# Three edits to the order in which results leave their PSUM banks in a two-layer encoder trunk

## The chip, the cores and the metric

The kernel runs on one core of one Trainium2 chip. The metric is the device time of one execution in microseconds (us); lower is better. The kernel before took 1122.87 us, the median of three runs (1122.69 to 1123.55).

## The reference

Two encoder layers work on x (512 tokens by 1024 features) in float32. Each layer normalises x by rows, projects it to queries, keys and values, lets every token attend to other tokens and to 256 memory rows, projects the heads back and adds the result to x; then comes a gated feed-forward block. The memory rows are normalised once, and each layer makes its own keys and values of them.

```python
mem_n = rms_norm(mem, mem_norm_g)
for i in range(DEPTH):                       # 2 layers
    h = rms_norm(x, g_mix_pre[i])
    proj = h @ w_in[i]                       # 12 query heads, 3 key and 3 value heads, 4 memory query heads
    tok = mixer_a(q, k, v, sink, ...) if i == 0 else mixer_b(q, k, v, qk_g, ...)
    mkv = mem_n @ w_mem_kv[i]                # 4 key heads and 4 value heads of 256 memory rows
    mo = memory_attention(qm, km, vm)
    o = jnp.concatenate([tok, mo], axis=-1) @ w_o[i]
    x = x + rms_norm(o, g_mix_post[i])
    h = rms_norm(x, g_ffn_pre[i])
    gu = h @ w_gate_up[i]
    f = (silu(gu[..., :D_FF]) * gu[..., D_FF:]) @ w_down[i]
    x = x + rms_norm(f, g_ffn_post[i])
```

Layer 0 (mixer A) turns a part of each key by position and limits attention to a band of tokens. Layer 1 (mixer B) normalises every query and key head by its own mean square, then turns it, and attends to all tokens.

## The kernel before, in words

**Numbers in two parts.** Every matmul operand is kept as two reduced float32 parts: a high part, made by a copy on ACT, and a low part, the difference of the source and the high part, made on DVE (`split`, lines 274 to 284; `split_scaled`, lines 286 to 293, also scales by a row factor r). A product is three matmuls: high by high, high by low, low by high (`mm3`, line 268).

**Who reads a bank.** Products and transposes end in PSUM banks. A bank is read by one engine at a time: where ACT and DVE both read it, the second waits for the first. A bank is free for TensorE (PE) again after the last reader.

**Order of the work.** PE issues in the order in which the program is traced. That order is a list written by hand, sorted by planned positions (`put` and `lay` in `mixer`, lines 659 to 740, with the constants `PACE`, line 37). The order on ACT, DVE, POOL and on SP, which issues all the loads, is chosen by the compiler: it plays the program through with modelled durations and, when an engine is free, takes the ready instruction that was traced first. Once chosen, each engine issues strictly in that order.

**The mixer's steps around the change.**

- `start` (line 1105) loads the inputs of layer 0 and sets up late steps: for x tiles 1 to 3 and for the two memory tiles (128 rows each), one call of `turned` and one of `factors`. `turned` (line 334) transposes one 128x1024 tile in two blocks of four 128x128 transposes; each block fills one of two banks with tag t (tile tp), and `split` then moves it into its high and low parts (mT for the memory). `factors` (line 324) squares the tile's two halves on ACT into a scratch tile (scr, tag tmp, two buffers) and makes the row factor.
- `kv_pieces` (line 452) makes keys and values of token tile t from one bank of 128x384. When the product is done it splits the values (vs, lines 471 and 286 to 293: a copy on ACT, the difference on DVE), then copies the keys on ACT (kx, line 473), turns them (`rope_a` or `rope_b`, on DVE, in layer 1 with a square on ACT and a factor on POOL), splits them (k, line 482) and copies the high part once more on POOL (line 402). `keys` (line 404) transposes them later.
- `q_pieces` (line 492) does the like for four query heads: copy qx on ACT (line 514 or 516), turn, split (q), transpose (line 534).
- `mem_pieces` (line 371) makes memory keys and values of tile m from a bank of 128x512: `split_scaled` for the keys (k), the POOL copy, `split_scaled` for the values (vm), so ACT, DVE, ACT, DVE read the bank in turn.

Layer 1 does not transpose the memory: layer 0 stores mT (line 688) and layer 1 loads it back (line 477, behind the kx copy on its queue).

Of the kernel before, what the change touches and what calls it, by code (L numbers as in the profile page):

```python
# [9 lines left out]
F32 = mybir.dt.float32  # L10
# [21 lines left out]
WPART = 2  # L32
BIG = 1e37
NFILL = 3
LOTS = ((0, 8), (8, 14), (14, 22))

PACE = [{'lag': 1.692, 'vlag': 0.479, 'jstep': 0.213, 'kstep': 0.375, 'klag': 0.742, 'qoff': [0.212, 0.126, 0.099], 'qlag': 1.02, 'late': 0.6, 'moff': -0.235, 'mdur': 0.562, 'mlag': 0.697, 'kw': [0, 0, 2, 0], 'mw': [2, 1, 1, 0], 'qw': [1, 0, 0, 1, 3, 3, 3, 3], 'hoff': 0, 'ow': [10.3, 10.8, 12.2, 13.2], 'ox': 11.4, 'od': 0.3, 'hstep': 0.872, 'hlag': 1.742, 'hjstep': 0.135, 'hvlag': 0.751, 'owm': [0, 0, 0, 0, 0, 0, 0, 0], 'q0step': 0.27, 'q0off': -0.032, 'q0lag': 0.919, 'm0off': -0.078, 'm0dur': 0.002, 'm0lead': 1.887, 'mlead': 1.201, 'qlead': 0.921, 'q0lead': 1.555, 'qstep': 1.002, 'tw': [0, 0, 0, 0, 0, 0, 0, 0], 'h2off': 0}, {'lag': 1.824, 'vlag': 0.535, 'jstep': 0.218, 'kstep': 0.777, 'klag': 1.715, 'qoff': [-0.027, -0.162, -0.027], 'qlag': 1.189, 'late': 2.15, 'moff': -0.088, 'mdur': 0.384, 'mlag': 1.205, 'kw': [0, 0, 0, 0], 'mw': [0, 0, 0, 0], 'qw': [0, 0, 0, 0, 0, 3, 1, 1], 'hoff': 0, 'ow': [10.2, 10.7, 12.2, 13.2], 'ox': 11.3, 'od': 0.3, 'hstep': 0.946, 'hlag': 1.847, 'hjstep': 0.295, 'hvlag': 0.568, 'owm': [0, 0, 0, 0, 0, 0, 0, 0], 'q0step': 0.718, 'q0off': -0.018, 'q0lag': 1.136, 'm0off': -1.059, 'm0dur': 0.171, 'm0lead': 2.465, 'mlead': 3.162, 'qlead': 1.895, 'q0lead': 1.42, 'qstep': 0.998, 'tw': [0, 0, 0, 0, 0, 0, 0, 0], 'h2off': 0.016}]
# [142 lines left out]
class Trunk:  # L180
# [93 lines left out]
    def split(self, hi, lo, src, pool=0):  # L274
# [8 lines left out]
        else:  # L283
            nc.vector.tensor_sub(lo, src, hi.bitcast(F32))  # L284

    def split_scaled(self, hi, lo, src, r, pool=0):

        nc = self.nc
        if pool & 2:
            nc.gpsimd.tensor_scalar(hi, src, r, 1.0, op0=OP.mult, op1=OP.mult)  # L290
        else:
            nc.scalar.activation(hi, src, AF.Copy, scale=r)
        nc.vector.scalar_tensor_tensor(lo, src, r, hi.bitcast(F32), op0=OP.mult, op1=OP.subtract)
# [35 lines left out]
        self.mean_square(xt[:, 512:], ss[:, 1:2], scratch())  # L329
        self.rstd2(r, e, ss[:, 1:2])  # L330

    def turned(self, h, his, los, t, nq=4):

        for b in range(2):
            tp = self.ps.tile([P, 4, P], F32, tag="t", name="tp", bufs=2)
            for k in range(4):
                self.nc.tensor.transpose(tp[:, k], h[:, (4 * b + k) * P:(4 * b + k + 1) * P], self.ident)
            k0 = 4 * b
            sl = (slice(None), slice(k0 % nq, k0 % nq + 4), slice(t * P, (t + 1) * P))
            self.split(his[k0 // nq][sl], los[k0 // nq][sl], tp)  # L340

    def scale_rows(self, rs, by_row=False):
# [27 lines left out]

    def mem_pieces(self, l, mk, put, x0, dx, lag, xw):

        w, ps = {}, []
        for u in range(4):
            self.unit(self.a["wm"][l, u], self.side(l, "mw", u), put=put, x=xw[u], dst=w, key=u,
                      g=self.gcol[:, 1, 2 * u:2 * u + 2])

        def prod(u, m):
            if u == 0:
                ps.append(self.tagged("s"))  # L380
            for k in (2 * u, 2 * u + 1):
                ms = (slice(None), k, slice(m * P, (m + 1) * P))
                c = slice((k % 2) * 512, (k % 2) * 512 + 512)
                self.mm3(ps[m], self.mT[:, 0][ms], self.mT[:, 1][ms], w[u][0][:, c], w[u][1][:, c],
                         k == 0, k == KD - 1)
            if u < 3:
                return
            kv = ps[m].rearrange("p (z h d) -> p z h d", z=2, d=HD)
            k2 = self.core.tile([P, 4, 3 * HD], F32R, tag="q2", name="k2", bufs=3)
            r = self.rm[:, m:m + 1]  # L390
            self.split_scaled(k2[:, :, :HD], k2[:, :, HD:P], kv[:, 0], r)
            self.again(k2)
            self.split_scaled(mk["v"][:, m, :, :HD], mk["v"][:, m, :, HD:], kv[:, 1], r)
            put(x0[3] + dx[3] + m * dx[3] / 2 + lag, lambda: self.keys(k2, mk["a"], mk["b"], m, 4))

        for u in range(4):
            for m in range(2):
                put(x0[u] + m * dx[u] / 2, lambda u=u, m=m: prod(u, m))
# [53 lines left out]
    def kv_pieces(self, l):  # L452
# [6 lines left out]
        def prod(t, st, u):  # L459
            self.ready(t)  # L460
            if u == 0:
                st["ps"] = self.tagged("acc" if t < 2 else "s")
            ps = st["ps"]
            for k in (2 * u, 2 * u + 1):
                c = slice((k % 2) * 384, (k % 2) * 384 + 384)
                self.mm3(ps[:, :384], self.hslice(0, k, t * P, t * P + P), self.hslice(1, k, t * P, t * P + P),
                         w[u][0][:, c], w[u][1][:, c], k == 0, k == KD - 1)
            if u == 3:
                kv = ps[:, :384].rearrange("p (z h d) -> p z h d", z=2, d=HD)
                r = self.rs[:, t:t + 1]  # L470
                self.split_scaled(self.vs[:, t, :, :HD], self.vs[:, t, :, HD:], kv[:, 1], r)
                kx = self.core.tile([P, 4, HD], F32, tag="qx", name="kx", bufs=3)
                ins = nc.scalar.activation(kx[:, :NG], kv[:, 0], AF.Copy, scale=r).ins
                if l:
                    with self.tc.issue_after(ins):
                        z, ks = t // 2, slice(t % 2 * 4, t % 2 * 4 + 4)
                        nc.sync.dma_start(self.mT[:, z, ks].bitcast(F32), self.spill[:, z, ks])
                r = self.rope(l, kx, t, NG, 1)
                if l:
                    nc.vector.tensor_mul(kx[:, :NG], kx[:, :NG], r[:, :NG, None].to_broadcast([P, NG, HD]))  # L480
                st["k2"] = self.core.tile([P, 4, 3 * HD], F32R, tag="q2", name="k2", bufs=3)
                self.split(st["k2"][:, :NG, :HD], st["k2"][:, :NG, HD:P], kx[:, :NG])
                self.again(st["k2"][:, :NG])
# [621 lines left out]
    def start(self, mkp):  # L1105
# [3 lines left out]
        with ExitStack() as st:  # L1109
# [41 lines left out]
            for t in range(1, NT):  # L1151
                late[t] = lambda t=t: (self.turned(x[t], *self.hT, t), factors(t, scr))
            for m in range(2):
                late["m", m] = lambda m=m: (self.turned(mh[m], [self.mT[:, 0]], [self.mT[:, 1]], m, KD),
                                            self.factors(mh[m], self.rm[:, m:m + 1], scr))
        return late

# [100 lines left out]
```

## Time and profile before

| what | value |
|---|---|
| median of three runs | 1122.87 us |
| the profiled execution, device time | 1122.94 us |
| its span, first to last instruction | 1121.1 us |
| PE busy | 1096.3 us, 98% of the span |
| DVE, ACT, POOL busy | 838.8, 660.6, 203.6 us |
| mixer of layer 0, with its start | about 0 to 170 us |
| mixer of layer 1 | about 545 to 757 us |
| granted TensorE clock | full in every slice |

The rest of the span is the two feed-forward blocks. Times below are microseconds from the start of the span. In a timeline, a row gives start, length, engine, source line, operation, tiles written and read, shape and count; a bracket at its end says how long the engine sat idle before it and what ended that.

### The profile page before, as it was taken

The numbers are of one execution on the slowest core, as the hardware profiler recorded it, in microseconds if no ns is written. First come the engines' busy times: TensorE is split into PE (matmuls) and PEld (weight loads), VectorE is DVE, ScalarE is ACT, GpSimd is POOL, SyncE is SP. The second block draws the span as 40 slices with busy tenths as digits, with TensorE's granted clock in tenths as the row PEclk, the third lists the DMA queues.
The fourth block names the chain that finished last, engine by engine and source line by source line (L and its number), as shares of the span: only waits on it lengthen the run. The fifth ranks groups of instructions, "written<-read, shape, count | busy, mean of one in ns | idle before, by whom it ended". The sixth has DMA issues, their size and how long they took to land.

```text
span 1121.1 us, 19499 instructions
## 1 busy us (share of the span) xinstructions
PE 1096.3 (98%) x7463; PEld 1005.2 (90%) x7463; DVE 838.8 (75%) x1399; ACT 660.6 (59%) x1343; POOL 203.6 (18%) x348
## 2 busy tenths in 40 slices
PE   9999999999999999999999999999999999999997
PEld 7899988899889989998898888878999899899985
DVE  5688885999547777885788988758995478669854
ACT  6678984666445634663467888756664355346631
POOL 5693331202000000000343552212000000000001
PEclk9999999999999999999999999999999999999999
DMA  6521015433753372325543221145136223422243
GB/s 237 198 84 40 20 57 215 161 132 118 242 178 113 118 278 76 113 78 196 179 151 113 76 76 39 38 164 175 46 107 210 73 79 113 147 66 101 84 165 113
DMA packets 38685, 139.29 MB, mean 124 GB/s; under 512 B 4416, under 2 KB 4800, under 8 KB 38464
## 3 DMA queue, kind: packets, MB, share of 16 engines
q1 hardware_dynamic: 38448, 137.91, 36.6%
q8 instruction: 58, 0.95, 0.3%
q14 instruction: 35, 0.29, 0.1%
q10 hardware_dynamic: 144, 0.14, 0.0%
HBM read 119.16 MB, written 18.87 MB: 123 GB/s over the span
## 4 chain that ended last, share of the span: by engine, by line
PE 70%; DVE 5%; ACT 3%; POOL 2%; issue 1%; DVEq 0%; POOLq 0%; ACTq 0%
PE ps L990 12%; PE ps L991 12%; PE ps L992 12%; PE ps L271 10%; PE ps L270 10%; PE ps L272 9%; PE tp L619 2%; PE o L634 1%; PE o L633 1%; PE s L558 1%; PE s L559 1%; POOL r L299 1%; DVE wlo L284 1%; ACT whi L280 1%; ACT junk L303 0%
## 5 line engine op out<-in xcount | busy, mean ns | idle before, releaser
L280 ACT ACTIVATE whi<-raw 128x1024 fp32r<-128x1024 f32 (+2 forms) x186 | 157.9, 863 | 183.2 <-PE ps L992 82.0
L284 DVE TENSOR_TENSOR wlo<-raw,whi 128x1024 fp32r<-128x1024 f32 (+2 forms) x178 | 175.4, 996 | 76.4 <-ACT whi L280 73.0
L990 PE MATMUL ps<-sf,whi 128*128 128x256 f32 x640 | 179.8, 281 | 0.2
L991 PE MATMUL ps<-sf,wlo 128*128 128x256 f32 x640 | 179.9, 281 | 0.0
L992 PE MATMUL ps<-sf,whi 128*128 128x256 f32 x640 | 179.8, 281 | 0.0
L270 PE MATMUL ps<-whi,f 128*128 128x512 f32 x352 | 137.2, 390 | 0.0
L271 PE MATMUL ps<-wlo,f 128*128 128x512 f32 x352 | 137.1, 390 | 0.0
L272 PE MATMUL ps<-whi,f 128*128 128x512 f32 x352 | 137.0, 389 | 0.0
L992 PE MATMUL ps<-a,whi 128*128 128x256 f32 x480 | 134.4, 280 | 0.0
L990 PE MATMUL ps<-a,whi 128*128 128x256 f32 x480 | 134.3, 280 | 0.0
L991 PE MATMUL ps<-a,wlo 128*128 128x256 f32 x480 | 133.9, 279 | 0.0
L990 PEld LDWEIGHTS ps<-sf,whi 128*128 128x128 f32 x640 | 121.1, 189 | 1.1 <-ACT p L996 0.6
L991 PEld LDWEIGHTS ps<-sf,wlo 128*128 128x128 f32 x640 | 121.3, 190 | 0.5
L992 PEld LDWEIGHTS ps<-sf,whi 128*128 128x128 f32 x640 | 121.4, 190 | 0.0
L308 POOL TENSOR_SCALAR e<-sso 128x1 f32<-128x1 f32 x8 | 3.4, 422 | 566.6 <-ACT junk L303 566.4
L270 PE MATMUL ps<-whi,hT 128*128 128x256 f32 (+1 forms) x320 | 98.8, 309 | 0.0
L271 PE MATMUL ps<-wlo,hT 128*128 128x256 f32 (+1 forms) x320 | 93.8, 293 | 2.4 <-DVE wlo L284 1.9
L609 POOL TENSOR_SCALAR p<-p,rd 128x256 f32<-128x256 f32 (+2 forms) x128 | 76.5, 619 | 99.6 <-DVE rd L606 41.9
L272 PE MATMUL ps<-whi,hT 128*128 128x256 f32 (+1 forms) x320 | 93.7, 293 | 0.0
L990 PEld LDWEIGHTS ps<-a,whi 128*128 128x128 f32 x480 | 90.4, 188 | 0.2
L991 PEld LDWEIGHTS ps<-a,wlo 128*128 128x128 f32 x480 | 90.4, 188 | 0.2
L992 PEld LDWEIGHTS ps<-a,whi 128*128 128x128 f32 x480 | 90.1, 188 | 0.0
(199 smaller groups left out, 2732.3 us busy)
## 6 DMA issues: line engine op xcount, KB each, us to landing
raw<-in_wgu_dram SPq DMA_DIRECT2D x48, 512.0 KB, 4.3
raw<-in_wd_dram SPq DMA_DIRECT2D x44, 512.0 KB, 4.5
rb<-in_wgu_dram SPq DMA_DIRECT2D x40, 512.0 KB, 3.6
raw<-in_wo_dram SPq DMA_DIRECT2D x17, 512.0 KB, 3.6
raw<-in_wq_dram SPq DMA_DIRECT2D x16, 512.0 KB, 4.8
xt<-x SPq DMA_DIRECT2D x12, 512.0 KB, 4.4
raw<-in_wm_dram SPq DMA_DIRECT2D x8, 512.0 KB, 3.8
x<-y SPq DMA_DIRECT2D x8, 512.0 KB, 3.0
```

The lines of the kernel that those rows point to most:

```text
L270: mm(out, lh, rh, start=first, stop=False)
L271: mm(out, lh, rl, start=False, stop=False)
L272: mm(out, ll, rh, start=False, stop=last)
L280: nc.scalar.activation(hi, src, AF.Copy)
L284: nc.vector.tensor_sub(lo, src, hi.bitcast(F32))
L299: g.tensor_tensor(r, r, self.mhalf[:, :r.shape[1]], op=OP.pow)
L558: nc.tensor.matmul(s[:, :n], qi, hd["ka"]()[:, k0 * P:k1 * P], start=True, stop=False)
L609: self.pooled = nc.gpsimd.tensor_scalar(hd["p"][z][:, :n], hd["p"][z][:, :n], rd[:, z:z + 1], 1.0, op0=OP.mult, op1=OP.mult)
L619: nc.tensor.transpose(tp[:, z], hd["p"][i][:, jj * P:(jj + 1) * P], self.ident)
L990: mm(out, wh[:, s], rh, start=start and k == 0, stop=False, skip_group_check=True)
L991: mm(out, wl[:, s], rh, start=False, stop=False, skip_group_check=True)
L992: mm(out, wh[:, s], rl, start=False, stop=k == 3, skip_group_check=True)
```

## The change

1. In `kv_pieces` the copy kx of the keys is traced ahead of the split of the values, in both layers, for all four token tiles.
2. In `mem_pieces` the two high parts (keys, values) are made first, both on ACT, and then the two low parts, both on DVE; the POOL copy is traced after all four. Both layers, two tiles each.
3. `turned` takes an argument `by`. For the two memory tiles it is the scratch allocator of `factors`: a copy on ACT, traced 150 places earlier in priority, moves the bank into a float32 scratch tile in SBUF, and both parts are then split from that tile. This adds four copies of 128x512 on ACT, in layer 0 only. No DMA is added or removed.

```diff
+URGENT = 150
+    def urgent(self):
+        return self.tc.high_priority(URGENT)

-    def turned(self, h, his, los, t, nq=4):
+    def turned(self, h, his, los, t, nq=4, by=None):
             sl = (slice(None), slice(k0 % nq, k0 % nq + 4), slice(t * P, (t + 1) * P))
+            if by is not None:
+                x = by().rearrange("p (k n) -> p k n", n=P)
+                with self.urgent():
+                    self.nc.scalar.activation(x, tp, AF.Copy)
+                tp = x
             self.split(his[k0 // nq][sl], los[k0 // nq][sl], tp)

     def mem_pieces(self, l, mk, put, x0, dx, lag, xw):
-            self.split_scaled(k2[:, :, :HD], k2[:, :, HD:P], kv[:, 0], r)
+            his, los = [k2[:, :, :HD], mk["v"][:, m, :, :HD]], [k2[:, :, HD:P], mk["v"][:, m, :, HD:]]
+            for z in range(2):
+                nc.scalar.activation(his[z], kv[:, z], AF.Copy, scale=r)
+            for z in range(2):
+                nc.vector.scalar_tensor_tensor(los[z], kv[:, z], r, his[z].bitcast(F32), op0=OP.mult, op1=OP.subtract)
             self.again(k2)
-            self.split_scaled(mk["v"][:, m, :, :HD], mk["v"][:, m, :, HD:], kv[:, 1], r)

     def kv_pieces(self, l):
-                self.split_scaled(self.vs[:, t, :, :HD], self.vs[:, t, :, HD:], kv[:, 1], r)
                 kx = self.core.tile([P, 4, HD], F32, tag="qx", name="kx", bufs=3)
                 ins = nc.scalar.activation(kx[:, :NG], kv[:, 0], AF.Copy, scale=r).ins
+                self.split_scaled(self.vs[:, t, :, :HD], self.vs[:, t, :, HD:], kv[:, 1], r)

     def start(self, mkp):
-                late["m", m] = lambda m=m: (self.turned(mh[m], [self.mT[:, 0]], [self.mT[:, 1]], m, KD),
+                late["m", m] = lambda m=m: (self.turned(mh[m], [self.mT[:, 0]], [self.mT[:, 1]], m, KD, scr),
                                             self.factors(mh[m], self.rm[:, m:m + 1], scr))
```

## Rows read from the trace of the kernel before

**Rows 1.** The profile's page, busy time by engine: PE.
```profile
PE 1096.3 (98%) x7463; PEld 1005.2 (90%) x7463; DVE 838.8 (75%) x1399; ACT 660.6 (59%) x1343; POOL 203.6 (18%) x348
```
**Rows 2.** Who PE waited for, whole span: us in total, times, longest us.
```profile
PE ps L271 <- DVE wlo L284: 1.9, 2, 1.1
...
PE tp L337 <- DVE mT L284: 1.4, 1, 1.4
...
PE tp L534 <- DVE q L284: 0.5, 1, 0.5
```
**Rows 3.** Timeline, layer 0, all engines: the memory's transposes and what surrounds them.
```profile
28.17 2.18 ACT L280 ACTIVATE whi<-raw 128x512 fp32r<-128x512 f32 x4
...
28.87 5.51 POOL L282 TENSOR_TENSOR wlo<-raw,whi 128x512 fp32r<-128x512 f32 x4
...
29.31 1.44 DVE L284 TENSOR_TENSOR k<-kx,k 128x192 fp32r<-128x192 f32 x1
...
30.25 1.06 ACT L280 ACTIVATE mT<-tp 128x512 fp32r<-128x512 f32 x2
30.86 1.29 DVE L284 TENSOR_TENSOR mT<-tp,mT 128x512 fp32r<-128x512 f32 x2
...
31.61 1.25 PE L337 MATMUL tp<-cst,mh 128*128 128x128 f32 x8 [1.40 <-DVE mT L284]
...
32.62 0.47 PE L270 MATMUL ps<-whi,mT 128*128 128x512 f32 x1
...
33.16 0.40 PE L272 MATMUL ps<-whi,mT 128*128 128x512 f32 x1
```
**Rows 4.** Timeline, layer 0: bank of token tile 2's keys and values.
```profile
24.55 0.42 ACT L292 ACTIVATE vs<-ps,rs 128x192 fp32r<-128x192 f32 x1 [0.48 <-PE ps L272]
...
25.45 0.42 ACT L473 ACTIVATE kx<-ps,rs 128x192 f32<-128x192 f32 x1
...
27.90 0.36 ACT L280 ACTIVATE k<-kx 128x192 fp32r<-128x192 f32 x1 [2.03 <-DVE kx L428]
```
**Rows 5.** Low parts (line 284) and float32 copies (line 153): ns min/median/max, first and last start us.
```profile
L284 DVE TENSOR_TENSOR k<-kx,k x8: 348/359/1437, 17.6 to 583.4; 128x192 fp32r<-128x192 f32 x8
L284 DVE TENSOR_TENSOR mT<-tp,mT x4: 676/686/693, 30.9 to 35.9; 128x512 fp32r<-128x512 f32 x4
...
L153 ACT ACTIVATE as<-tp x8: 586/598/616, 199.4 to 771.8; 128x512 f32<-128x512 f32 x8
```
**Rows 6.** Chain of waits, layer 1, 548 to 615 us: start us, us, what.
```profile
563.53 0.42 ACT vs L292
563.95 0.32 ACT kx L473
...
579.27 0.33 DVE vs L293
...
595.33 0.69 DVE wlo L284
```
**Rows 7.** Timeline, layer 1, ACT.
```profile
561.75 0.43 ACT L292 ACTIVATE vs<-ps,rs 128x192 fp32r<-128x192 f32 x1
...
575.55 0.41 ACT L292 ACTIVATE vs<-ps,rs 128x192 fp32r<-128x192 f32 x1
...
579.64 0.42 ACT L473 ACTIVATE kx<-ps,rs 128x192 f32<-128x192 f32 x1
...
583.23 0.46 ACT L514 ACTIVATE qx<-ps,rs 128x256 f32<-128x256 f32 x1
```
**Rows 8.** Timeline, layer 1: DVE's low parts of weights, PE's products.
```profile
571.13 2.90 DVE L293 SCALAR_TENSOR_TENSOR wlo<-raw,cst,whi 128x512 fp32r<-128x512 f32 x4 [0.17 <-ACT whi L292]
...
573.28 0.39 PE L271 MATMUL ps<-wlo,mT 128*128 128x512 f32 x1
...
581.80 0.28 PE L272 MATMUL ps<-whi,hT 128*128 128x256 f32 x1
```
**Rows 9.** Timeline, layer 0, ACT: the last square of a memory half.
```profile
21.48 0.64 ACT L303 ACTIVATE scr<-mh 128x512 f32<-128x512 f32 x1
```

More of the change, by code (lines that the diff above doesn't have):

```diff
@@ L371, in mem_pieces @@
     def mem_pieces(self, l, mk, put, x0, dx, lag, xw):
+        nc = self.nc
         w, ps = {}, []
```

## The prediction

> **What bounds the kernel now.** I read the page first: PE is busy 1096.3 of 1121.1 us [rows 1], so all that a change of order can win is PE's idle time, some 25 us over the whole span, and only the part of it that hangs on the moved instructions. So the second view is the list of who PE waited for. Three of its entries touch the moved work [rows 2]: 1.4 us, once, in which a transpose waits for a low part of mT; 1.9 us, two waits for low parts of weights, the longer one 1.1 us; and 0.5 us in which a transpose waits for a query's low part. The third view is the timeline around each, to see who was late, and the fourth the chain of waits in layer 1.
>
> The first wait stands in layer 0. PE has filled both banks with the first memory tile's transposes and cannot start the second tile's until DVE has read the first bank (the 1.40 us) [rows 3]. The bank was full long before. Its ACT copy stood behind four weight copies, which run from 28.17 to 30.35, and only then follow mT's high parts at 30.25 and its low parts at 30.86. Those weight copies are themselves late: ACT sat idle for 2.03 us before the key copy that stands ahead of them [rows 4], because the keys were turned late.
>
> In layer 1 the chain that ends in the wait for a weight's low part at 595.33 comes out of the keys: it passes a copy of values on ACT (0.42 us), the copy of keys behind it, and a low part of values on DVE (0.33 us) [rows 6].
>
> **Edit 1, keys first.** No instruction is added. In layer 0 the key copy of tile 2 starts at 25.45, 0.90 us after the bank could first be read at 24.55: it stands behind the values' copy and, as the bank has one reader at a time, behind their low part on DVE [rows 4]. Keys first, it can start 0.90 us earlier, and so can the turn, the key's high part and the weight copies behind it. No wait of PE ends at these keys; the 0.90 us counts only in edit 3. The values' own parts come 0.42 us later; what hides it is the query products, which all stand ahead of the first head that reads values.
>
> In layer 1 the same order costs more: tile 0's values leave at 561.75, but its keys only at 563.95, since ACT had been given the next tile's values in between [rows 6, 7]; tile 3's values leave at 575.55 and its keys at 579.64, 4.1 us later [rows 7]. DVE is nearly full there, so not all of that comes back. What certainly leaves the chain are the two steps on values, 0.42 + 0.33 = 0.75 us [rows 6]. What can come back at most before the next thing is late: the first query copy starts at 583.23, and its product ends about 581.80 + 0.28 = 582.08 [rows 7, 8]; so 1.15 us. I take the middle, 0.9 us off PE's waits. Bounds: 0, if POOL's factor or DVE's order sets the chain anyway, and 1.6 us, the 1.1 us and the 0.5 us waits whole [rows 2]. Next late thing: the query chains, one after the other on ACT.
>
> **Edit 2, the memory's high parts first.** Four banks, the same four instructions each. ACT no longer waits for DVE between its two copies, and the keys' low part comes one copy later: 0.46 us, by the query copy of the same 128x256 (the last row) [rows 7]. PE transposes these keys only after further query products, which are the cover; without it 0.46 us per tile would show. PE's list of waits has none for these parts. I count 0, and 0.5 us either way for the range.
>
> **Edit 3, the memory's rows leave by a copy.** Four copies of 128x512 into float32 are added on ACT, 0.598 us each by the nearest row [rows 5], 2.4 us together. With them a bank is free after one ACT instruction instead of an ACT and a DVE instruction. If ACT reaches it only at 30.25 as now, the bank is free at 30.85 instead of 31.55 (30.86 + 0.69): 0.7 of the 1.40 us go. With the 0.90 us of edit 1, or with the copies' priority ahead of one or two of the four weight copies, all 1.40 us go.
>
> But the wait has a successor: PE's first product with mT starts at 32.62, its third matmul, at 33.16, 0.54 us later, reads the low part [rows 3]. The path to it is now copy, copy, high part, low part: 3 x 0.60 + 0.69 = 2.5 us from when ACT turns to it. From 29.35 (30.25 less 0.90) the low part ends at 31.84, so the product may start at 31.3, a gain of 1.3 us. From 30.25 it ends at 32.74, and the gain is 0.4 us.
>
> The low part is also made from another place. Now one of its two operands is in PSUM, and all four took 0.68 to 0.69 us although POOL was busy beside them [rows 3, 5]. The low part of the keys, whose two operands are both in SBUF, took 0.36 us as a rule, and 1.44 us at 29.31, under the same POOL pieces [rows 3, 5]. The Trainium skill (SBUF — State Buffer, section Who interferes with whom) says that a DVE instruction with two SBUF inputs contends with a GpSimd instruction that reads SBUF, that whoever starts first holds the shared port for its whole instruction, and that with at most one SBUF input there is no contention; by that rule all four new low parts are exposed, which speaks against this edit, and the trace agrees as far as the 1.44 us goes. POOL's four pieces here are 5.51 / 4 = 1.38 us each [rows 3]. One low part behind a whole piece ends 1.38 us later: from 29.35 at 33.2, and the product starts at 32.7, a loss of 0.1 us; from 30.25, a loss of 1.0 us. With undisturbed low parts the whole sum (with layer 1's 0.9 us) would be 1120.7 us; with one POOL piece ahead of each, 1122.1 us.
>
> So the edit is worth between -1.4 and +1.0 us; I take -0.6, halfway between the 1.3 us gain and the 0.1 us loss from 29.35, since edit 1 makes that start the likely one. The moved squares of the memory rows (below) I count at 0. A gain at 32 us reaches the end because PE is the bound nearly everywhere behind it.
>
> **The sum**: -0.6 - 0.9 + 0 = -1.5 us against the profiled execution's 1122.94 us (its span of 1121.1 and 1.8 us around it), so 1121.4 us. That execution stands 0.07 us above the median of the runs. About 0.2% of the time, 2.25 us, is what a measurement of this kernel can tell from no change; so 1120.6 to 1125.1 counts as the same.
>
> **Rivals.**
>
> *Both waits go whole* (chance 0.31). The copies overtake the weight copies, low parts meet no POOL piece, and keys come early enough to clear the query transposes too: -1.4 - 1.6 - 0.5 = -3.5 us, 1119.4 us. For it: the keys of tile 3 have 4.1 us to win [rows 7]. Against: the longer mT path, and DVE, which has little room around 575 us.
>
> *Each wait gets a successor* (0.21). The product waits for mT as long as the transposes waited for the bank, and in layer 1 POOL's factors and DVE's order set the chain's end: 0, so 1122.9 us. This is also how it looks if the scheduler, which plays the program with modelled durations, puts the instructions back where they were, so that the change does not do what it says.
>
> *Slower: the low parts meet POOL* (0.12). Place: layer 0, 30 to 38 us. In the worst order three low parts in a row (both blocks of the first memory tile, the first of the second) each wait for one of the four POOL pieces: high part done at 30.25 + 1.8 = 32.05, then 3 x (1.38 + 0.69) = 6.2 us, so 38.3. The second tile's product, six matmuls of 0.27 us behind the first [rows 3], needs it at 32.62 + 1.6 + 0.54 = 34.8. PE stands still for 3.5 us; with layer 1's -0.9 that is +2.6, 1125.5 us. It decides from when the second tile's first low part ends after 34.8. For it: the 1.44 us row. Against: the keys' median stayed at 0.36 us [rows 5], and POOL, once delayed, is out of the way sooner than in this worst order. It is what the rule of the Trainium skill named above would give if it held three times in a row.
>
> Two smaller ones I fold into these. The squares of the memory rows end at 22.1 now [rows 9], and they share their two buffers with the new copies; handed out in traced order, they would wait for the low parts and put four squares of 0.64 us, 2.6 us of ACT work, into 31 to 38 us. And in layer 1 the four low parts of memory weights run from 571.13 to 574.03, the first needed by 573.28 [rows 8]: at 0.73 us each, the first is done at 571.86, so 1.4 us of key work can go ahead of them free, and more shows in PE one to one.
>
> **How the numbers follow.** My forecast has 0.36. With the successor rival's 0.21 the time is the same with 0.57; faster by over 0.2% 0.31; slower 0.12. The likeliest case's own range, from its bounds, is 1120.6 to 1122.9. For 8 in 10 the range goes down to 1118.9, half a microsecond under the whole gain, as orders elsewhere shift too, and up to 1124.2, the worst of edit 3's ordinary bounds (+1.0) with edit 2's 0.5 against and nothing won in layer 1, less 0.2 us, as the three seldom meet.
>
> **What would show it.** Right: the transposes at about 30 us start without the 1.40 us wait; each bank of the memory is read by ACT alone; the first product with mT starts 0.3 to 1.3 us earlier; kx starts as the product ends in all eight banks; the wait at 595 us is shorter. Step by step wrong: a wait of the mT product for low parts as long as the old one (edit 3), low parts of mT above 0.69 us (the port), the wait at 595 us unchanged although the keys are early (edit 1), a new wait near 573 us, squares of the memory rows after 30 us. The forecast as a whole is wrong if PE's idle time changes in the heads or the feed-forward blocks, where nothing is edited, by more than it does here.

## The result, and the profile after

The kernel after takes 1127.97 us (median of six runs), the kernel before, run beside it, 1122.91 us: a ratio of 1.0047, 95% interval 1.0037 to 1.0056, so 5.1 us slower. The prediction said 1121.4 us, range 1118.9 to 1124.2. It is wrong in sign, and the result lies outside its range. The profiled execution took 1127.67 us, with a span of 1125.7 us against 1121.1.

The page's row of busy times by engine, to be set beside [rows 1]:

```profile
PE 1097.7 (98%) x7463; PEld 1005.7 (89%) x7463; DVE 839.7 (75%) x1399; ACT 662.4 (59%) x1347; POOL 202.3 (18%) x348
```

ACT has its four instructions more (1347 instead of 1343). PE is busy 1.4 us longer with the same 7463 instructions: some of them were slower. The list of who PE waited for, whole span (us in total, times, longest us), against [rows 2]:

```profile
PE ps L271 <- ACT mT L281: 5.4, 1, 5.4
...
PE ps L272 <- DVE wlo L285: 1.3, 2, 0.8
...
PE ps L273 <- DVE mT L285: 0.2, 1, 0.2
```

The 1.4 us wait of the transposes is gone and so is the 0.5 us wait of the query's transposes. The weights' low parts cost 1.3 instead of 1.9 us. But there is a wait that was nowhere before: 5.4 us, once, in which a product waits for a *high* part of mT, made by ACT. The timeline of layer 0, all engines, shows where it comes from; its first rows answer to [rows 3].

```profile
27.06 2.20 ACT L281 ACTIVATE whi<-raw 128x512 fp32r<-128x512 f32 x4 [0.40 <-PE ps L273]
...
28.16 6.44 POOL L283 TENSOR_TENSOR wlo<-raw,whi 128x512 fp32r<-128x512 f32 x4
...
29.16 1.06 ACT L348 ACTIVATE scr<-tp 128x512 f32<-128x512 f32 x2
...
29.80 1.13 PE L342 MATMUL tp<-cst,mh 128*128 128x128 f32 x8
30.12 1.15 ACT L281 ACTIVATE mT<-scr 128x512 fp32r<-128x512 f32 x2
30.78 2.69 DVE L285 TENSOR_TENSOR mT<-scr,mT 128x512 fp32r<-128x512 f32 x2 [0.69 <-ACT mT L281]
...
30.89 0.47 PE L271 MATMUL ps<-whi,mT 128*128 128x512 f32 x1
...
31.83 0.50 PE L273 MATMUL ps<-whi,mT 128*128 128x512 f32 x1 [0.23 <-DVE mT L285]
...
32.63 0.40 PE L273 MATMUL ps<-whi,mT 128*128 128x512 f32 x1
33.39 1.27 DVE L439 TENSOR_TENSOR rt<-kx,cst 128x48 f32<-128x48 f32 x1
33.86 0.61 ACT L308 ACTIVATE scr<-mh 128x512 f32<-128x512 f32 x1
...
34.47 0.61 ACT L308 ACTIVATE scr<-mh 128x512 f32<-128x512 f32 x1
...
35.08 1.05 ACT L348 ACTIVATE scr<-tp 128x512 f32<-128x512 f32 x2
...
37.52 0.36 ACT L281 ACTIVATE k<-kx 128x192 fp32r<-128x192 f32 x1 [1.07 <-DVE kx L442]
37.79 1.13 ACT L281 ACTIVATE mT<-scr 128x512 fp32r<-128x512 f32 x2
...
38.43 1.29 DVE L285 TENSOR_TENSOR mT<-scr,mT 128x512 fp32r<-128x512 f32 x2 [0.16 <-ACT mT L281]
...
38.45 0.80 PE L271 MATMUL ps<-whi,mT 128*128 128x512 f32 x1 [5.43 <-ACT mT L281]
...
39.05 0.63 PE L272 MATMUL ps<-wlo,mT 128*128 128x512 f32 x1
```

The first memory tile goes as the prediction had it: the copies come off at 29.16, the second tile's transposes start at 29.80 without a wait (31.61 before), and the first product starts at 30.89 instead of 32.62. Then the *second* tile, whose transposes are done by 30.93, stands still. Its copies run only at 35.08, behind four weight copies (32.24 to 33.95) and two squares (scr<-mh) that lay before 22.1 us in the kernel before [rows 9]. Its high parts run only at 37.79, behind the keys' high part (37.52), which waited for DVE to turn the keys. PE starts the second tile's product at 38.45.

The products behind the wait are slow: 0.63 us each instead of 0.40. The same kernel's busy time by stretch (stretch in us, its length, busy time and count of PE, PEld, DVE, ACT, POOL, granted TensorE clock, DMA share, GB/s) says why:

```profile
34.00:38.00 4.00, 0.00 (x0) 0.00 (x0) 3.87 (x9) 2.93 (x9) 3.28 (x7) 0.76 0.40 140
...
38.00:42.00 4.00, 3.55 (x8) 2.78 (x9) 1.57 (x3) 2.79 (x7) 1.41 (x4) 0.50 0.90 328
42.00:43.00 1.00, 1.00 (x4) 0.77 (x3) 0.00 (x0) 0.62 (x2) 0.83 (x1) 0.55 0.62 262
43.00:45.00 2.00, 2.00 (x12) 1.66 (x11) 0.00 (x0) 0.06 (x1) 1.71 (x2) 1.00 1.17 492
```

While PE had nothing to do, its granted clock fell to 0.50, the 1.2 GHz level, and it stayed there through 38 to 42 us of products; from 43 us it is 2.4 GHz again.

In layer 1 the change did what it should. The timeline there, ACT and PE, against [rows 7, 8]:

```profile
581.02 0.41 ACT L486 ACTIVATE kx<-ps,rs 128x192 f32<-128x192 f32 x1
...
588.64 0.47 ACT L528 ACTIVATE qx<-ps,rs 128x256 f32<-128x256 f32 x1 [0.69 <-PE ps L273]
...
600.95 0.39 PE L272 MATMUL ps<-wlo,hT 128*128 128x256 f32 x1 [0.53 <-DVE wlo L285]
```

The whole program is some 6.3 us late at that point. So the keys of tile 3, at 581.02, come 4.9 us earlier than before (579.64 + 6.3 - 581.02), and the first query copy 0.9 us earlier (583.23 + 6.3 - 588.64).

PE's 7463 instructions come in the same order in both kernels, so each can be set beside itself. The difference in start time grows and shrinks as follows: -0.43 us before the memory's transposes (the start of the program, no work of the change), -1.38 where their wait is gone, +0.48 at the first product's low part, +5.70 at the second tile's high part, +1.95 during the slow products, -1.43 in layer 1 (nearly all of it at two places, near 592 and 596 us of the kernel before), -0.30 in many small steps behind. The sum is +4.59 us, the 4.6 us of the spans. Such differences compare one execution of each kernel.

### The profile page after: what moved, and what is told of

It is laid out like the page before. It is cut to its first block, busy times and chain, and to the rows that moved or that the text cites. A ratio compares the mean times of both kernels' runs of the same rounds, so it can differ in the third digit from the quotient of the medians.

```text
span 1125.7 us, 19514 instructions
## 1 busy us (share of the span) xinstructions
PE 1097.7 (98%) x7463; PEld 1005.7 (89%) x7463; DVE 839.7 (75%) x1399; ACT 662.4 (59%) x1347; POOL 202.3 (18%) x348
## 4 chain that ended last, share of the span: by engine, by line
PE 69%; DVE 5%; ACT 2%; POOL 2%; issue 2%; DMA 1%; POOLq 0%; DVEq 0%; SPq 0%; ACTq 0%
PE ps L1004 12%; PE ps L1006 12%; PE ps L1005 12%; PE ps L272 10%; PE ps L271 10%; PE ps L273 10%; PE tp L633 2%; PE o L648 1%; PE o L647 1%; PE s L572 1%; PE s L573 1%; POOL r L304 1%; DVE wlo L285 1%; POOL p L623 0%; ACT whi L281 0%
```

## The experiments

The first two take the change apart.

**Edits 1 and 2 without edit 3.** The memory's rows are split from their banks again:

```diff
-late["m", m] = lambda m=m: (self.turned(mh[m], [self.mT[:, 0]], [self.mT[:, 1]], m, KD, scr),
+late["m", m] = lambda m=m: (self.turned(mh[m], [self.mT[:, 0]], [self.mT[:, 1]], m, KD),
```

> Edits 1 and 2 alone, the memory tiles split from their banks as before. All theories: the 5.4 us wait for mT goes, since nothing stands between the bank and the parts. The bank wait of 1.4 us comes back, but shorter, about 0.7 us, because the weight copies already ran 1.1 us earlier (27.06 against 28.17). If the 1.4 us won in layer 1 belong to the key order, they stay: 1122.9 - 0.7 - 1.4 = 1120.8 us. If they came only from layer 0 being late, the time is 1122.2 us or more.

Measured: 1121.55 us, ratio 0.9991 [0.9981, 1.0000]. Who PE waited for between 27 and 44 us:

```profile
PE tp L342 <- DVE mT L285: 1.1, 1, 1.1
PE ps L273 <- DVE mT L285: 0.6, 1, 0.6
```

The time lies between the two forecasts. The old bank wait is back, 0.3 us shorter, with a 0.6 us successor; by PE's start times layer 0 is some 0.5 us worse than before, and layer 1 gains its 1.5 us without the copies.

**Edit 3 alone.** The kernel before, with the copies and the argument `by` of the change and nothing else of it:

```diff
-late["m", m] = lambda m=m: (self.turned(mh[m], [self.mT[:, 0]], [self.mT[:, 1]], m, KD),
+late["m", m] = lambda m=m: (self.turned(mh[m], [self.mT[:, 0]], [self.mT[:, 1]], m, KD, scr),
```

> Edit 3 alone, keys and memory rows as before. Theory buffers (the second memory tile's copies wait for scratch buffers that the squares of the first tile hold, and those wait for the first tile's low parts): the wait of PE is there without edits 1 and 2, 5.4 us or up to 0.9 us more since the keys come later, and layer 1 wins nothing: 1129 to 1130.5 us. If the wait needs the new key order (ACT standing behind a key part), it is under 3 us and the time under 1126.

Measured: 1128.56 us, ratio 1.0057 [1.0043, 1.0071]. Who PE waited for between 27 and 44 us:

```profile
PE ps L271 <- ACT mT L281: 3.9, 1, 3.9
```

The loss comes with edit 3 alone, and layer 1 gains nothing. The wait lies between the two forecasts. The keys' high part is not ahead of the second tile's here (it is behind it, at 38.08), and 3.9 us of wait remain; the squares are at 34.16 and 34.77 and the copies at 35.38, as in the change.

**Edit 2 alone.** The kernel before, with the order of `mem_pieces` of the change and nothing else of it:

```diff
-self.split_scaled(k2[:, :, :HD], k2[:, :, HD:P], kv[:, 0], r)
+his, los = [k2[:, :, :HD], mk["v"][:, m, :, :HD]], [k2[:, :, HD:P], mk["v"][:, m, :, HD:]]
+for z in range(2):
+    nc.scalar.activation(his[z], kv[:, z], AF.Copy, scale=r)
+for z in range(2):
+    nc.vector.scalar_tensor_tensor(los[z], kv[:, z], r, his[z].bitcast(F32), op0=OP.mult, op1=OP.subtract)
 self.again(k2)
-self.split_scaled(mk["v"][:, m, :, :HD], mk["v"][:, m, :, HD:], kv[:, 1], r)
```

> The kernel before with edit 2 alone: both high parts of a memory tile ahead of both low parts; nothing is left out. Theory (that order is hidden under the products, as the prediction counted it): no wait over 0.5 us new, within 0.6 us of before, 1122.4 to 1123.4. Rival (part of layer 1's gain or of the loss is its): a change of 0.8 us or more.

Measured: 1122.80 us, ratio 1.0002 [0.9993, 1.0011]; PE's start times keep their distance to the kernel before within 0.3 us from 9 to 233 us and within 0.4 us from 347 to 830 us. No cost can be told from none.

**Keys first in layer 1 alone.** The kernel before, with this in `kv_pieces`:

```diff
-self.split_scaled(self.vs[:, t, :, :HD], self.vs[:, t, :, HD:], kv[:, 1], r)
+if not l:
+    self.split_scaled(self.vs[:, t, :, :HD], self.vs[:, t, :, HD:], kv[:, 1], r)
 kx = self.core.tile([P, 4, HD], F32, tag="qx", name="kx", bufs=3)
 ins = nc.scalar.activation(kx[:, :NG], kv[:, 0], AF.Copy, scale=r).ins
+if l:
+    self.split_scaled(self.vs[:, t, :, :HD], self.vs[:, t, :, HD:], kv[:, 1], r)
```

> The kernel before with edit 1 in layer 1 alone: keys ahead of the values' parts there, layer 0, memory's order and the bank reads as before; nothing is left out. Theory (layer 1's 1.4 us gain is the keys' order alone, and layer 0 gained nothing from any edit): TensorE's waits before 580 us as before, the two q transpose waits near 585 to 592 us gone and the low-part wait near 595 about half, so 1.2 to 1.6 us less than before: 1121.0 to 1121.7. Rival (layer 1's gain needs layer 0's or memory's changes): within 0.3 us of before.

Measured: 1121.35 us, ratio 0.9986 [0.9977, 0.9995], as the theory had it: 1.4 us below the kernel before. PE's start times fall back by 0.9 us at the query transposes near 592 us and by 0.65 us at the weights' low part near 595. Who PE waited for between 575 and 605 us:

```profile
PE ps L272 <- DVE wlo L285: 0.5, 1, 0.5
```

The change has the same row there; before there were 1.1 and 0.5 us [rows 2]. Layer 1's gain needs the keys' order there and nothing else.

The rest asks what the 5.4 us wait is made of.

**The clock.** In the change, 22 products of 512 columns that nothing uses are put on PE ahead of the second tile's product; they write a bank that its first product then starts afresh:

```diff
+if l == 0 and (u, m) == (0, 1):
+    for _ in range(22):
+        nc.tensor.matmul(ps[1], self.mT[:, 0, 0, :P], w[0][0][:, :512], start=True, stop=True)
```

> The changed kernel with 22 more matmuls of 512 columns whose results are written over, put where PE stands still for 5.4 us (22 x 0.213 = 4.7 us, so they fit). They compute nothing that is used. If the slow products behind the wait (0.43 us apart instead of 0.23, 38.5 to 42.5 us) come from PE's clock having dropped in the wait, they run at full clock and the time falls by about 1.9 us, to 1126.0 us. If they are slow for another reason, 1128 us.

Measured: 1125.75 us, ratio 1.0031 [1.0018, 1.0043]. Busy time by stretch:

```profile
36.00:38.00 2.00, 2.00 (x10) 1.50 (x8) 1.97 (x6) 0.98 (x3) 1.75 (x4) 1.00 0.70 244
38.00:42.00 4.00, 3.52 (x15) 2.44 (x14) 1.72 (x4) 3.64 (x9) 1.75 (x6) 1.00 0.76 262
```

The second tile's product starts as late as in the change (38.71), but the clock holds. Against the kernel before, run beside it, this version is 3.3 us slower, the change 5.1: 1.8 us of the loss are the clock, and the start times set side by side had said 1.95.

**Squares ahead of copies, tile by tile.** For each memory tile `factors` is traced ahead of `turned`:

```diff
-late["m", m] = lambda m=m: (self.turned(mh[m], [self.mT[:, 0]], [self.mT[:, 1]], m, KD, scr),
-                            self.factors(mh[m], self.rm[:, m:m + 1], scr))
+late["m", m] = lambda m=m: (self.factors(mh[m], self.rm[:, m:m + 1], scr),
+                            self.turned(mh[m], [self.mT[:, 0]], [self.mT[:, 1]], m, KD, scr))
```

> All three edits, but the squares of each memory tile traced ahead of its transposes, so that they come first at the two scratch buffers. Theory buffers: squares end before 23 us as in the kernel before, the second tile's copies start when its transposes end, about 31 us, PE waits for mT less than 1 us, its clock stays full: 1122.9 - 1.4 (bank) - 1.4 (layer 1) + 0.5 = about 1120.6 us. Theory port (low parts of two SBUF operands beside POOL's pieces, 0.84 and 1.78 us, hold PE up): the second tile's low part still ends near 35 us, a wait of about 2 us, 1122.5 us. Theory ACT load (four more copies are too much there): 1124 us or more.

Measured: 1128.00 us, ratio 1.0051 [1.0039, 1.0064], a miss. The first tile's squares went back to 18.6 and 19.8 us, but the second tile's are traced behind the first tile's copies, ran at 34.03 and 34.65, and its copies at 35.26; PE waited 5.7 us. That the buffers are handed out in traced order is borne out; that it was the first tile's squares that did the harm is not.

**All squares ahead of all copies.**

```diff
-late["m", m] = lambda m=m: (self.turned(mh[m], [self.mT[:, 0]], [self.mT[:, 1]], m, KD, scr),
-                            self.factors(mh[m], self.rm[:, m:m + 1], scr))
+late["m", m] = lambda m=m: ([self.factors(mh[z], self.rm[:, z:z + 1], scr) for z in range(2 - 2 * m)],
+                            self.turned(mh[m], [self.mT[:, 0]], [self.mT[:, 1]], m, KD, scr))
```

> The change with the squares of both memory tiles traced ahead of the first tile's copies, so that no square stands between the copies of the two tiles in the ring of two scratch buffers; nothing is left out. Theory A (the ring alone: the second tile's copies wait for squares that wait for the first tile's low parts): all four squares lie before 24 us, the second tile's copies leave at about 33 us instead of 35.08, its high part follows at 34 to 35, TensorE's one long wait falls from 5.4 to 2 to 3 us and the clock fall behind it mostly goes: 1123.5 to 1125. Theory B (the order on ACT: whatever the squares do, the second tile's high part stands in ACT's program behind the keys' high part, which waits at 37.5 for the rotated keys from a late DVE): the wait stays at 4.5 to 5.5 us and the clock falls as before: 1127 to 1128. Theory C (the low parts of SBUF copies beside POOL are the bound): a wait for DVE's mT takes its place, 1125 to 1127.

Measured: 1128.20 us, ratio 1.0047 [1.0030, 1.0064]. Timeline, ACT:

```profile
33.75 1.06 ACT L348 ACTIVATE scr<-tp 128x512 f32<-128x512 f32 x2
...
37.32 0.36 ACT L281 ACTIVATE k<-kx 128x192 fp32r<-128x192 f32 x1 [1.40 <-DVE kx L442]
37.59 1.13 ACT L281 ACTIVATE mT<-scr 128x512 fp32r<-128x512 f32 x2
```

The copies come 1.3 us earlier, and it is of no use: the high part still stands behind the keys' high part, which waits for DVE. PE's wait is 4.7 us, as theory B said; the time is a little above B's 1128.

**High and low parts at the front of their engines' orders, as the copies are.** In `turned`, inside `if by is not None`:

```diff
-                tp = x
+                with self.urgent():
+                    self.split(his[k0 // nq][sl], los[k0 // nq][sl], x)
+                continue
```

> The change with the two parts of the memory rows put at the front of their engines' orders as the copies are, so that on ACT the second tile's high part stands right behind its copies and ahead of the values' and keys' high parts; nothing is left out. Theory A (ring): the copies still leave at 35 us, so the high part comes at 36.1 instead of 37.8; the long wait falls from 5.4 to about 3.7 us and the time by 1.7 to 3 us, according to whether the clock still falls: 1125 to 1126.3. Theory B (the order on ACT is the greater part): the wait falls by more than 2.5 us and the time to 1124 or less. Theory C (port, DVE): the high part comes earlier, but TensorE then waits as long for DVE's low part: 1127 to 1128.

Measured: 1127.52 us, ratio 1.0037 [1.0024, 1.0050]. The wait is 3.7 us, as theory A said, with the high part at 36.19 directly behind the copies at 35.23. But the time is above A's 1126.3, and the distance to the kernel before fell only from 5.1 to 4.5 us: the products that start earlier run at the lower clock (0.50 in 38 to 42 us, and 0.71 on the mean of 42 to 43).

**A buffer of its own for each copy.** The copies go to four buffers that only the heads use, much later; the squares are back before 24 us:

```diff
-x = by().rearrange("p (k n) -> p k n", n=P)
+x = self.core.tile([P, 4, P], F32R, tag="th", name="th", bufs=4).bitcast(F32)
```

> The change with each of the four copies in a buffer of its own (four that the heads use only later), so that copies and squares share nothing; nothing is left out. Theory A (the ring): no copy waits for a buffer, all four are done by 32 us, the squares are where they were before the change (before 24 us), the long wait falls to 1 to 2 us, clock 1.0: 1121.5 to 1124. Theory B (the order on ACT behind the keys' high part): the second tile's high part now stands ahead of that part in ACT's order, so B also gives a shorter wait, but by that order and not by the buffers. Theory C (port): the first tile's low parts stay near 1.3 us each beside POOL's split, against 0.69 from the bank, and TensorE waits 1 to 2 us for DVE's mT: 1123 to 1125. The kernel with no copies took 1121.55; A alone would give that or 0.5 us better.

Measured: 1127.49 us, ratio 1.0039 [1.0024, 1.0054], above the times of theories A and C; B gave none. Timeline, ACT:

```profile
31.18 1.08 ACT L348 ACTIVATE th<-tp 128x512 f32<-128x512 f32 x2
33.03 1.71 ACT L297 ACTIVATE whi<-raw,cst 128x256 fp32r<-128x256 f32 x4 [0.76 <-DMA raw<-in_wq_dram]
...
35.77 1.14 ACT L281 ACTIVATE mT<-th 128x512 fp32r<-128x512 f32 x2
```

The second tile's copies run at 31.18, against 33.75 with the squares out of the way but two buffers for the four copies. But ACT, which plays its instructions in a fixed order, has four weight copies (33.03, behind 0.76 us of waiting for their DMA) and the values and keys of tile 3 ahead of the second tile's first high part (35.77). PE waits 2.6 us for it and 0.9 us more for a low part, which DVE starts at 37.84, behind the turning of tile 3's keys and the values' low part; and the clock falls.

**Both cures together.** Own buffers, and both parts at the front.

> Both earlier cures at once: each copy in a buffer of its own, and the two parts of the memory rows at the front of their engines' orders; nothing is left out. Each cure alone left one link of the wait standing (own buffers 2.6 + 0.9 us of waits, front of the order 3.7 us) and the clock fell in both. Theory now held (the wait has several links in series on ACT, ring, order behind weights and keys, and only without all of them does it go; the clock follows the wait): the second tile's high part comes at 33.5 to 34.5 us, TensorE's waits before it sum to 1 to 2 us, the granted clock stays 1.0 in 36 to 43 us, and the time is 1121 to 1123. Rival (the copies' ACT work and the slow low parts beside POOL are enough by themselves): waits of over 2.5 us stay, the clock falls, 1125.5 or more.

Measured: 1123.79 us, ratio 1.0011 [1.0002, 1.0021]. Who PE waited for between 27 and 44 us, then busy time by stretch:

```profile
PE ps L273 <- DVE mT L285: 2.0, 2, 1.5
PE ps L271 <- ACT mT L281: 0.7, 1, 0.7
```

```profile
38.00:42.00 4.00, 4.00 (x14) 3.20 (x13) 2.57 (x4) 1.77 (x4) 2.98 (x3) 0.70 0.93 389
42.00:43.00 1.00, 1.00 (x11) 0.98 (x10) 0.51 (x3) 0.53 (x2) 0.07 (x1) 1.00 1.08 344
```

The waits are 0.7 us for ACT and 2.0 us for DVE's low parts, above the theory's 1 to 2 us; the time lies between theory and rival. The first two low parts take 1.48 us each beside POOL's pieces, two weight pieces behind them 0.95 us each. The profiled execution took 1125.23 us, and its clock falls for some 3 us. The mean granted clock of each of the eleven executions tells that most did not lose it: it is 0.998 or 0.999, as in the kernel before, in the seven of 1122.86 to 1124.52 us, and 0.996 or 0.997 in the four of 1125.07 to 1125.62 us.

**And two of POOL's four pieces taken away.** As the last, with `'mw': [2, 0, 0, 0]` for `[2, 1, 1, 0]` in layer 0's entry of `PACE`. This takes two units of the memory's weights off POOL, which had scaled them and made their low parts; ACT and DVE make both parts now. So two of POOL's four pieces beside the first low parts are gone, and so are its later pieces (35.68 and 39.34 in the last kernel).

> As the kernel with own buffers and urgent parts, and the low parts of the one memory weight unit that POOL computed beside DVE's low parts of the copies go to DVE; nothing is left out. Theory (the SBUF reads of DVE slow each other beside POOL's): the low parts from the copies take 0.68 to 0.75 us each instead of 0.84 to 1.8, at no POOL split beside them. Rival (the SBUF source alone makes them slow, or ACT's traffic does): they stay over 1 us. For the time: DVE gets some 2 to 3 us more weight work before them, so 1120.5 to 1123.5 by either.

Measured: 1122.65 us, ratio 1.0002 [0.9993, 1.0011]. POOL is done at 32.35 us. The durations of DVE's low parts of mT in this kernel (ns min/median/max, first and last start):

```profile
L285 DVE TENSOR_TENSOR mT<-th,mT x4: 677/681/692, 32.5 to 35.5; 128x512 fp32r<-128x512 f32 x4
```

in the change:

```profile
L285 DVE TENSOR_TENSOR mT<-scr,mT x4: 685/841/1776, 30.8 to 39.0; 128x512 fp32r<-128x512 f32 x4
```

and in the next kernel, which reads the bank:

```profile
L285 DVE TENSOR_TENSOR mT<-tp,mT x4: 675/676/678, 30.6 to 35.7; 128x512 fp32r<-128x512 f32 x4
```

Read from SBUF, a low part is as fast as from the bank where POOL is not at work, and up to 2.6 times as long where it is. In the profiled execution the granted clock is 1.00 from 34 to 46 us. Who PE waited for between 27 and 44 us, and the timeline of DVE:

```profile
PE ps L273 <- DVE mT L285: 1.4, 1, 1.4
PE ps L271 <- ACT mT L281: 0.5, 1, 0.5
```

```profile
26.94 4.28 DVE L298 SCALAR_TENSOR_TENSOR wlo<-raw,cst,whi 128x512 fp32r<-128x512 f32 x4 [0.52 <-POOL whi L295]
31.14 1.43 DVE L285 TENSOR_TENSOR k<-kx,k 128x192 fp32r<-128x192 f32 x1
32.49 1.28 DVE L285 TENSOR_TENSOR mT<-th,mT 128x512 fp32r<-128x512 f32 x2
...
37.22 0.20 DVE L440 TENSOR_TENSOR rt<-kx,cst 128x48 f32<-128x48 f32 x1
```

The two waits are more than the single 1.4 us of the kernel before, and by PE's start times layer 0 is 1.2 us worse than before, while layer 1 gains its 1.5: the copies win nothing here either. The 1.4 us has a new link, though. DVE's first low part stands behind four low parts of weights, two of them taken over from POOL, and the keys' low part, held up beside POOL's last piece. What the copies would be worth without that isn't shown.

**No copies, parts at the front.** Edits 1 and 2, both parts of the memory's rows read the bank but stand at the front.

> Edits 1 and 2 with no copy: both parts of the memory rows read the bank as before the change, but are put at the front of their engines' orders as the copies are in the change. Nothing is left out. Theory A (the loss comes from the copies, that is ring, extra ACT work, and SBUF reads beside POOL): no wait for mT over 1 us, clock 1.0, low parts at 0.69 us each, time 1120.5 to 1121.8, as with edits 1 and 2 alone (1121.55). Rival (the loss comes from putting work of the memory rows at the front at all, which pushes the keys' work back): a new wait for the keys' or weights' parts of over 1 us and 1123 or more.

Measured: 1122.25 us, ratio 0.9994 [0.9985, 1.0004], the profiled execution 1121.79: a little above theory A's range. Waits of 1.1 and 0.6 us, as without the priority, where A had none above 1 us; the rival's new wait is not there. Its low parts at 30.59 run beside POOL's four pieces (28.73 to 34.28) at 0.68 us each.

In one table, by the waits of PE for mT or its banks in 27 to 44 us and the granted clock in 38 to 42 us; each ratio is to the kernel before as run beside that kernel:

| kernel | copies | waits, us | clock | median, us | ratio to before |
|---|---|---|---|---|---|
| the change | shared buffers | 5.4 + 0.2 | 0.50 | 1127.97 | 1.0047 |
| edit 3 alone | shared buffers | 3.9 | 0.50 | 1128.56 | 1.0057 |
| squares first, tile by tile | shared buffers | 5.7 | 0.52 | 1128.00 | 1.0051 |
| all squares first | shared buffers | 4.7 + 0.5 | 0.52 | 1128.20 | 1.0047 |
| parts at the front | shared buffers | 3.7 + 0.2 | 0.50 | 1127.52 | 1.0037 |
| own buffers | own | 2.6 + 1.4 | 0.50 | 1127.49 | 1.0039 |
| both | own | 0.7 + 2.0 | 0.70 | 1123.79 | 1.0011 |
| both, fewer POOL pieces | own | 0.5 + 1.4 | 1.00 | 1122.65 | 1.0002 |
| edits 1 and 2, no copies | none | 1.1 + 0.6 | 1.00 | 1121.55 | 0.9991 |
| the same, parts at the front | none | 1.1 + 0.6 | 1.00 | 1122.25 | 0.9994 |
| keys first in layer 1 alone | none | 1.4 | 1.00 | 1121.35 | 0.9986 |

## Why the prediction was wrong

**Edit 1, right.** -0.9 us in layer 1 (bounds 0 and -1.6): measured -1.43 in the change and -1.53 with that edit alone in that layer. The expected next late thing, the query chains, is the next late thing: the query copy comes only 0.9 us earlier although the keys came 4.9, and the chain that ends in the wait left at 600.95 us runs through three query chains, in each of which POOL's factor is the longest step (1.20 to 1.21 us). In layer 0, where 0 was counted without the copies, edits 1 and 2 cost some 0.5 us by PE's start times; edit 2 alone costs nothing, so it is likely the keys. Keys first in layer 0 alone was not run, and the times (ratios 0.9991 and 0.9986, intervals that overlap) don't tell the two kernels apart.

**Edit 2, right.** 0 forecast; the ratio is 1.0002, 1 within 0.1%.

**Edit 3, wrong: -0.6 us forecast, between -1.4 and +1.0; measured +6.75 us** at the memory (-1.38 + 0.48 + 5.70 + 1.95). The first half of the step held: the 1.40 us bank wait went whole, the four weight copies ahead of the bank copies start at 27.06 instead of 28.17, and the first product starts 1.7 us earlier (0.4 of it from the start of the program). It also named the successor at the third matmul, which came to 0.23 us. The step that failed is the one behind it: "The path to it is now copy, copy, high part, low part" follows the first tile only, and "The moved squares of the memory rows (below) I count at 0" sets aside a thing that ties the second tile to it. The first of the two small rivals I folded in held a part of the mechanism: "handed out in traced order, they would wait for the low parts and put four squares of 0.64 us, 2.6 us of ACT work, into 31 to 38 us". The squares did move there (two at 33.86 and 34.47; the other two only from 39.16). I had priced it as ACT *work*; it is a *wait*: four copies and four squares take turns at only two buffers, so the second tile's copies come behind the first tile's low parts and two squares. The squares account for the smaller share: with them out of the way the copies still run only at 33.75, with own buffers at 31.18, and in the change at 35.08. Nor did ACT stand idle for the low parts: they were done by 33.47, while ACT was busy with weight copies until the squares.

The runs show that this ring is one link of several, in series. Taken away alone (own buffers) it leaves 2.6 + 1.4 us, because ACT still has weights, values and keys ahead of the second tile's high part. The order taken away alone leaves 3.7 us. With both gone, 0.7 us for ACT and 2.0 for DVE remain, and with less work for POOL 0.5 and 1.4, the latter behind DVE's added work. Buffers alone or order alone is worth 0.6 us of the time, squares alone nothing, and the intervals don't tell 0.6 us from nothing. The next link stands right behind each, and the clock takes back what the wait gives.

**The slower rival had the place and the sign, but not the price.** It put 3.5 us of standing still at the second memory tile, 32 to 38 us, and 1125.5 us in all, chance 0.12. The wait was there, 5.4 us, but PE waited for ACT's high part and not, as in the rival, for a low part. The rival's mechanism, low parts held up by POOL, is one of the links: [rows 3] had 1.29 us for two low parts from the bank, after the change it is 2.69 for two beside POOL and 1.29 for two once POOL had finished that stretch. POOL's own four pieces took 6.44 instead of 5.51 us. Other DVE work is slow there too, the 128x48 step of the keys' turn with 1.27 us at 33.39, but that is not the copies' doing: with edits 1 and 2 and no copies two such steps took 0.99 and 1.22 us, at 32.14 and 33.17. The Trainium skill (SBUF — State Buffer, section Who interferes with whom) has the rule: two SBUF inputs contend with a GpSimd instruction that reads SBUF, one does not. The trace agrees on both halves, 1.34 us a low part from SBUF and 0.68 from the bank beside the same four pieces. I argued against it by the keys' median of 0.36 us; that median is over eight low parts, six of them with no low part of a weight on POOL beside them, and says nothing of the one stretch where there is.

**No term for the clock.** Neither the sum nor a rival had a price for what a long wait does to the work behind it. It was 1.8 to 1.95 us here.

**Sums.** The rival in which both waits go whole counts the query transposes' 0.5 us twice, since it is already in the 1.6 us of edit 1's bound; it comes to 1119.9 us, and the lower end of the range half a microsecond below that to 1119.4. The bounds given for the three edits add up to 1119.4 to 1124.4 us, not to the 1120.6 to 1122.9 called the likeliest case's own range. The measured time lies above all of these.

**What was seen beforehand.** Of the signs that were to show each step wrong, two turned up: low parts above 0.69 us, and squares of the memory rows after 30 us. A third did in part: the mT product waits longer than the transposes had, but for a high part. None of the others did: the wait at 595 us halved, there is no new wait near 573 us, and PE's idle time in the heads and feed-forward blocks changed by 0.3 us in all. Of the signs of being right, one was seen in part: the copy of tile 3's keys starts 1.2 us behind its product in layer 0 (29.97 to 31.16) and 1.3 us in layer 1 (579.72 to 581.02).

## What to carry to other kernels

A copy that frees a bank takes a buffer in exchange: before it is counted as free, list who else takes buffers of that tag, in traced order, and what the last reader of each waits for. Follow a moved step to the *next* tile on the same engines, not only to the first instruction that reads its result, and write down what stands between the two in the engine's fixed order. A median over a whole kernel does not price an instruction in one crowded stretch: take the row from that stretch.

## What the runs showed of the hardware

A wait of 2.6 to 5.7 us of TensorE was followed by products at 0.50 of the clock in every kernel that had one and nothing on PE to fill it, and the time at which full clock came back did not move with the start of the products. They began at 38.45, 38.26, 36.86 and 36.44 us (the change, all squares first, parts at the front, own buffers); full clock came back between 41.5 and 43 us in all four. With edit 3 alone they began at 37.31 and full clock came back at 44 (that execution took 1130.24 us, 1.7 above the median of its kernel). What sets this time isn't shown. So three kernels that cut the wait by 0.7 to 2.8 us were all within 0.7 us of the change. Waits that sum to 1.4 to 1.9 us, in the kernel before, in the one with fewer POOL pieces and in those without copies, left the clock at 1.00; three waits that sum to 2.7 us, the longest 1.5 (own buffers with parts at the front), did not. The Trainium skill (TensorE: Matmul & The Clock Gate, section What's actually happening) says that the lower clock is the default and activity lifts it; the rows at 0.50 behind each long wait, and the filled wait at 1.00, agree with that.

The size of POOL's effect on short instructions was a surprise: 1.27 us for a step of 48 columns which took 0.20 us where POOL was idle (at 37.22 in the kernel with fewer POOL pieces), against 1.34 and 0.68 us for a low part of 512 columns. Beside POOL's pieces the price was not in proportion to a DVE instruction's own length.
